# Gated linear attention in batches and a merge by branches, in a hybrid mixer block

## The chip, the cores and the metric

One core of a Trainium2 chip runs the whole block. The metric is the device time of one execution in microseconds (us), the median over several runs. Below, PE is TensorE (matmuls), ACT is ScalarE, DVE is VectorE, POOL is GpSimd, SP is SyncE, which here only issues loads.

## The reference, cut to what matters

512 tokens of width 1024 go through one layer. The input norm gives `h`; four branches are computed from `h @ w_in`, merged, and followed by an MLP.

```
merged = 0
for i in range(4):
    gate = sigmoid(h @ w_gate[i] + b_gate[i])               # 1024 x 1024 each
    merged = merged + gate * (branches[i] @ w_branch_up[i]) # 256 x 1024 each
x = x + rms_norm(merged @ w_out, norm_mix_post)
# branch 2, gated linear attention: 4 heads, 8 chunks of 64 tokens, 32 key channels, 64 value channels
attn = where(lower, q_in @ k_in.T, 0)          # within a chunk
o_c = attn @ v_c + q_in @ state                # per chunk
state = state * decay[:, None] + k_tail.T @ v_c
```

Branch 0 is a gated delta rule, branch 1 latent attention, branch 2 gated linear attention, branch 3 attention with forget gates ("forgetting attention"). Branches 0 and 2 end in a norm per head times an output gate. Everything is float32.

## The kernel before, in words

Activations are kept transposed, [128 channels, 512 tokens]. To keep float32 accuracy with faster matmuls, both sides of a projection are split into a high and a low part (`split`, L149 on ACT and L150 on DVE), and `mm3` (L246) makes three matmuls: hi*hi, hi*lo, lo*hi. A projection of 1024 channels onto 128 (`proj`) so has 24 matmuls of 128x512 columns, into one of two PSUM banks `acc`. Weights come through SP's queue into `raw` (four buffers of [128, 1024]) and are split into `whi`, `wlo` (three buffers each). Other PSUM work takes turns in six banks, b0 to b5; `banks["ring"]` says which of them a stage may use, and `ps_sm` takes the next one.

The order on each engine is not the order of the code. A scheduler at build time takes, for each engine, the earliest line of the program that its own model of the time finds ready, with a free buffer. So work that stands late in the code, as the gates' projections, fills TensorE while an earlier stage waits.

The stages, in the order of the code: input norm; projections for branch 0; its recurrence; other projections; two of the merge's gates (`gates(G0)`); inverses of 32x32 blocks; output gates; forgetting attention (`attention`, L757 logits, L770 transposes, L777 times v, L779 copy out); gated linear attention (L790 to L843); latent attention; merge (L933 to L962); output projection, second norm, MLP.

In gated linear attention, L801 makes `k_in q_in` for each head (32 rows of the array; one head after the other, each masked by L803 into a tile `gat`). Then a loop over the eight chunks follows: for an even chunk L820 multiplies `gat` with v (64 columns a head), L824 spreads the state of the four heads to a block matrix on DVE, L827 multiplies it with `q_in`, L832 makes `k v` of the chunk (64 rows, 32 columns a head), L838 updates the state on DVE, and after an odd chunk L842 copies the outputs. A float32 matmul is issued as two TensorE instructions, so counts in the trace are twice those of the code.

The merge first splits all eight outputs `brT` into hi and lo (`brh`, `brl`). Then it goes over the eight blocks m of 128 output channels. For each it has four gates (`gates`, at most 11 ahead, five places in `keep`, six in `gp2`), loads the block's columns of all four `w_branch_up` (512 KB), and for each branch makes six matmuls into a bank, multiplies by the gate (L957, DVE), and adds on POOL (L959, L961). The sum is split into `mh`, `ml`. `rowproj` then loads `w_out` in eight blocks of 128 rows; its blocks 3 to 6 are split into buffers that lie where the merge's memory was, so they wait for `ph1.close()`.

Of the kernel before, what the change touches and what calls it, by code (L numbers as in the profile page):

```python
# [25 lines left out]
NGATE = (5, 6)  # L26
# [9 lines left out]
# columns of w_in  # L36
# [5 lines left out]
# columns of the constants  # L42
# [10 lines left out]
# columns of the per-channel vectors  # L53
# [4 lines left out]
def constants():  # L58
# [19 lines left out]
    # rows of the row tile: 0-3 q norm, 4-7 k norm, 36-39 chunk tail, 96-99 fox, 100-103 gate, 104-107 beta  # L78
# [27 lines left out]
    # rows of the stacked row tile: 0-31 norms hi, 32-63 norms lo, 64-95 gates lo, 96-127 gates hi  # L106
# [14 lines left out]
def hybrid_mixer_kernel(ctx, tc, I, out):  # L121
# [8 lines left out]

    def ps_acc():
        return psp.tile([P, 512], F32, name="acc", tag="acc", bufs=2)
# [19 lines left out]
    # the tensor engine's clock rises with use  # L152
# [46 lines left out]
    def sumsq(ps, lhsT, src, t, first, last):  # L199
        """ps += lhsT.T @ src**2, the square in two parts"""  # L200
        sq, hi, lo = t("sq"), t("sqh", F32R), t("sql", F32R)
        act.activation(out=sq, in_=src, func=AF.Square)
        split(hi, lo, sq)
        pe.matmul(out=ps, lhsT=lhsT, rhs=hi, start=first, stop=False)
        pe.matmul(out=ps, lhsT=lhsT, rhs=lo, start=False, stop=last)
# [88 lines left out]
    def rows_4k(c0, a):  # L294
        """[128, 4, 256] of w_in"""
# [25 lines left out]
    def fslot(i, name, dt=F32):  # L321
        """the places of the keys and queries of FOX, then of GLA's tiles, then of the branches' high parts"""
# [8 lines left out]
    def bslot(name, dt=F32):  # L331
        return keep.tile([P, S], dt, name=name, tag="brT", bufs=8)

    brT = {i: [bslot("brT") for p in range(2)] for i in (0, 2)}
# [7 lines left out]
    def selector(kind, i):  # L342
        """one-hot rows against all 128 outputs (kind 0, 1: head i) or each half's head (2, 3: pair i)"""
# [9 lines left out]
    # token layout: gla_v | fox_v  # L353
# [11 lines left out]
    def silu(dst, src):  # L365
        """dst = src * sigmoid(src)"""
# [6 lines left out]
    def softplus(dst, z, rows):  # L373
        """dst = max(z, 0) + log1p(exp(-|z|)) on the given partitions"""
# [4 lines left out]
        # series for small arguments  # L379
# [26 lines left out]
    # rows: 0-31 kpe, 32-63 kpe with its halves swapped, 64-79 gla_lr, 96-99 fox_f, 100-103 dn_a, 104-107 dn_b  # L406
# [48 lines left out]
    # A^T and (q k)^T per head, [key, (tile, query)]  # L455
# [35 lines left out]
    # decayed q, transposed, in the place of q  # L491
# [8 lines left out]
    # token layout: k times beta and decay, v times beta (in the places of k and v), k times tail decay  # L500
# [14 lines left out]
    def gate_proj(bi, zc0):  # L515
        """silu of the projected output gate"""
        for p, wt in enumerate(stat_tiles(w_in, zc0, 256)):
            psz = proj(wt, hh, hl)
            z = brT[bi][p]
# [29 lines left out]
    gts = []  # L549

    def gslot(n):
        """the place of the n-th gate"""
        early = n % sum(NGATE) < NGATE[0]
        return (keep if early else gp2).tile([P, S], F32, name="gate", tag="gate0" if early else "gate1",
                                             bufs=NGATE[not early])

    def gates(upto):
        for n in range(len(gts), min(upto, 4 * KD)):
            m, i = n // 4, n % 4
            ps = proj(w_split(raw_cols(I["w_gate"][0, i], P * m)), hh, hl)  # L560
            g = gslot(n)
            with tc.high_priority():
                act.activation(out=g, in_=ps, func=AF.Exp, scale=-1.0, bias=vecn(8 * i + m))
            act.activation(out=g, in_=g, func=AF.Ln, bias=1.0)
            act.activation(out=g, in_=g, func=AF.Exp, scale=-1.0)
            gts.append(g)

    gates(G0)
    # inverses of the diagonal 32x32 blocks of I + A^T, half of a block's columns to a partition
    half = [slice(C * e, C * e + C) for e in range(2)]  # L570
    za = [bslot("za")[:, 0:256 * (e + 1)].rearrange("p (s c) -> p s c", c=16) for e in range(2)]
# [25 lines left out]
    XC = [bslot("XC").rearrange("p (g c) -> p g c", c=32) for z in range(2)]  # L597
# [7 lines left out]
    brT.update({i: [bslot("brT") for p in range(2)] for i in (3, 1)})  # L605
    # (I + A)^-1 transposed, from the inverses of its 32-blocks
# [4 lines left out]
    def times_at(h, src):  # L611
        """the chunks' products, one above the other"""
# [37 lines left out]
    # recurrence over chunks; the state is kept block diagonal for each pair of heads  # L650
# [43 lines left out]
    def head_norm(bi, gain_row, oT):  # L694
        """rms norm over each head's channels, times the gate"""
        for p in range(2):
# [6 lines left out]
            dve.tensor_tensor(out=brT[bi][p], in0=brT[bi][p], in1=sq, op=ALU.mult)  # L703

    # gated linear attention: gates, decayed queries and keys
# [45 lines left out]
    def attention(ap, p, qT, kT, rows, scale, mask, vt, bi, sb, tb):  # L751
        for j in range(NT):
# [26 lines left out]
            act.copy(out=brT[bi][p][:, j * P:n], in_=psb[:, 0:P])  # L779

    # forgetting attention: 64 channels, then the rows (f_q, 1) against (1, -f_k)
# [5 lines left out]
    gp = fp  # L787
    GT = ("oG0", "gat0", "gat1", "gat2", "gat3", "oG1")

    def gt_(name):  # L790
        return fslot(GT.index(name), name)

    at = []
    for h in range(H):
        hs = slice(32 * h, 32 * h + 32)
        a_ = gt_(f"gat{h}")
        pool.memset(a_, 0.0)
        ps = ps_sm()
        for j in range(NT):
            js = slice(j * P, (j + 1) * P)  # L800
            pe.matmul(out=ps[:, js], lhsT=k_in[hs, js], rhs=q_in[hs, js], start=j == 0, stop=j == NT - 1,  # L801
                      skip_group_check=True, tile_position=(32 * h, 0))
        dve.copy_predicated(out=a_.rearrange("p (j c) -> p j c", c=P),  # L803
                            mask=cv("inc").bitcast(I32).unsqueeze(1).broadcast_to([P, NT, P]),
                            data=ps.rearrange("p (j c) -> p j c", c=P))
        at.append(a_)

    oG = [gt_("oG0"), gt_("oG1")]
# [3 lines left out]
    for n in range(NCH):  # L812
        j, o = n // 2, n % 2
        rs = slice(C * o, C * o + C)
        cur, nxt = Sg[n % 2], Sg[(n + 1) % 2]
        if o == 0:
            pso = ps_sm()
            for h in range(H):
                p, e = h // 2, h % 2
                pe.matmul(out=pso[C * e:C * e + C, p * P:(p + 1) * P], lhsT=vtok[0][:, j, C * h:C * h + C],  # L820
                          rhs=at[h][:, j * P:(j + 1) * P], start=h < 2, stop=False, skip_group_check=True)
        if n > 0:
            sm_ = gp.tile([P, 256], F32, name="Smask", tag="Smask", bufs=2)
            dve.tensor_tensor(out=sm_.rearrange("p (h c) -> p h c", c=C), in0=cur.unsqueeze(1).broadcast_to([P, H, C]),  # L824
                              in1=cv("bd32").rearrange("p (h c) -> p h c", c=C), op=ALU.mult)
            for p in range(2):
                pe.matmul(out=pso[:, p * P + C * o:p * P + C * o + C], lhsT=sm_[:, p * P:(p + 1) * P],  # L827
                          rhs=q_in[:, C * n:C * n + C], start=False, stop=o == 1 and p == 1, skip_group_check=True)
        if n < NCH - 1:
            psk = ps_sm()  # L830
            for h in range(H):
                pe.matmul(out=psk[32 * h:32 * h + 32, 0:C], lhsT=ktg[rs, j * P + 32 * h:j * P + 32 * h + 32],  # L832
                          rhs=vtok[0][rs, j, C * h:C * h + C], start=True, stop=True, skip_group_check=True,
                          tile_position=(C * o, 32 * h))
            if n == 0:
                dve.tensor_copy(out=nxt, in_=psk[:, 0:C])
            else:
# [291 lines left out]
```

## Time and profile before

| | |
|---|---|
| three runs, us | 912.97, 908.45, 916.18 |
| median, us | 912.97 |
| profiled execution: its span, us | 906.0 |
| TensorE busy | 891.2 us, 98% |
| VectorE, ScalarE, GpSimd busy | 49%, 43%, 13% |
| chain that ended last | 94% TensorE |
| moved by DMA | 83.30 MB |

The profile gives the profiled execution's time as its span, from its first to its last instruction; the median of the runs is 7.0 us above it. In the chain, 57% of the span are the matmuls of L246 into `acc` and 24% those into the other banks.

### The profile page before, as it was taken

The page shows a single profiled execution, that of the slowest core. Times are in us where ns is not written, and L with a number is a line of the kernel's source. Part 1 is how long each engine was busy: PE and PEld are TensorE (multiplying, and loading weights), DVE is VectorE, ACT ScalarE, POOL GpSimd, SP SyncE. Part 2 cuts the span into 40 slices and gives each one's busy share as a digit, 9 for nine tenths or more (in the row PEclk, how much of TensorE's full clock was granted, in tenths as well). Part 3 has the DMA queues.
Part 4 walks back from the last instruction along what each step waited for, and adds up shares of the span by engine and source line. Part 5 has one row for each costly group of instructions (what it writes and reads, how often), then busy time and mean ns, then how long its engine had stood idle before and what let it go on. Part 6 is the DMA issues. An engine that isn't in the chain of part 4 may idle for free.

```text
span 906.0 us, 11146 instructions
## 1 busy us (share of the span) xinstructions
PE 891.2 (98%) x4407; PEld 724.1 (80%) x4407; DVE 443.2 (49%) x717; ACT 393.4 (43%) x685; POOL 113.5 (13%) x96
## 2 busy tenths in 40 slices
PE   7999999999999999999999999999999999999997
PEld 6987788877667777888888789888888888888885
DVE  6378797436866775443336467322222233333324
ACT  6346453423886764445543355333222333222222
POOL 3100020100000002221124200422332200000000
PEclk9999999999999999999999999999999999999999
DMA  7333244501121012333333732333333333323202
GB/s 261 105 94 93 58 93 110 118 24 39 55 60 47 26 53 67 112 93 94 93 95 92 237 87 70 115 96 94 93 95 102 130 116 94 93 93 94 93 1 93
DMA packets 123699, 83.30 MB, mean 92 GB/s; under 512 B 19488, under 2 KB 115760, under 8 KB 123648
## 3 DMA queue, kind: packets, MB, share of 16 engines
q1 hardware_dynamic: 117696, 77.03, 29.5%
q10 hardware_dynamic: 5696, 4.73, 1.7%
q0 software_dynamic: 256, 0.85, 0.3%
q8 instruction: 34, 0.56, 0.2%
q14 instruction: 17, 0.14, 0.1%
HBM read 79.69 MB, written 2.88 MB: 91 GB/s over the span
## 4 chain that ended last, share of the span: by engine, by line
PE 94%; DVE 2%; ACT 1%; DMA 1%; POOL 1%; issue 0%; ACTq 0%; DVEq 0%; POOLq 0%
PE acc L246 57%; PE b L246 24%; PE b L757 2%; PE b L777 2%; PE b L278 1%; PE b L469 1%; PE b L770 1%; DMA raw<-in_w_out_dram 1%; PE b L616 1%; PE b L673 1%; PE b L801 1%; PE b L678 1%; POOL gate L959 1%; PE b L665 1%; PE b L646 0%
## 5 line engine op out<-in xcount | busy, mean ns | idle before, releaser
L150 DVE TENSOR_TENSOR wlo<-raw,whi 128x1024 fp32r<-128x1024 f32 x134 | 172.8, 1293 | 264.2 <-ACT whi L149 263.9
L149 ACT CAST whi<-raw 128x1024 fp32r<-128x1024 f32 x136 | 142.4, 1050 | 272.4 <-PE acc L246 238.7
L246 PE MATMUL acc<-hl,whi 128*128 128x512 f32 x416 | 165.4, 398 | 0.0
L246 PE MATMUL acc<-hh,whi 128*128 128x512 f32 x416 | 165.2, 397 | 0.0
L246 PE MATMUL acc<-hh,wlo 128*128 128x512 f32 x416 | 164.1, 394 | 0.0
L246 PE MATMUL acc<-h2l,whi 128*128 128x512 f32 (+1 forms) x240 | 91.8, 383 | 0.0
L246 PE MATMUL acc<-h2h,whi 128*128 128x512 f32 (+1 forms) x240 | 91.8, 382 | 0.0
L246 PE MATMUL acc<-h2h,wlo 128*128 128x512 f32 (+1 forms) x240 | 91.7, 382 | 0.0
L246 PEld LDWEIGHTS acc<-hl,whi 128*128 128x128 f32 x416 | 78.4, 188 | 16.6 <-issue 1.2
L246 PEld LDWEIGHTS acc<-hh,whi 128*128 128x128 f32 x416 | 78.2, 188 | 16.2 <-issue 1.1
L246 PEld LDWEIGHTS acc<-hh,wlo 128*128 128x128 f32 x416 | 78.2, 188 | 15.6 <-issue 0.4
L246 PE MATMUL b<-wlo,whi 128*128 128x512 f32 x192 | 74.8, 389 | 0.0
L246 PE MATMUL b<-whi 128*128 128x512 f32 x192 | 74.8, 389 | 0.0
L246 PE MATMUL b<-whi,wlo 128*128 128x512 f32 x192 | 74.7, 390 | 0.0
L246 PEld LDWEIGHTS acc<-h2h,whi 128*128 128x128 f32 x240 | 45.1, 188 | 8.8
L246 PEld LDWEIGHTS acc<-h2h,wlo 128*128 128x128 f32 x240 | 45.1, 188 | 8.7
L246 PEld LDWEIGHTS acc<-h2l,whi 128*128 128x128 f32 x240 | 45.1, 188 | 8.6
L959 POOL TENSOR_TENSOR gate<-gate 128x512 f32<-128x512 f32 x16 | 22.6, 1416 | 189.2 <-DVE gate L957 189.2
L246 PEld LDWEIGHTS b<-whi,wlo 128*128 128x128 f32 x192 | 36.1, 188 | 7.8 <-DVE wlo L150 0.4
L246 PEld LDWEIGHTS b<-wlo,whi 128*128 128x128 f32 x192 | 36.1, 188 | 7.5
L246 PEld LDWEIGHTS b<-whi 128*128 128x128 f32 x192 | 36.1, 188 | 7.4
L1035 POOL TENSOR_TENSOR u<-u 128x512 f32<-128x512 f32 x16 | 25.7, 1604 | 110.3 <-ACT u L1034 110.1
(312 smaller groups left out, 1413.8 us busy)
## 6 DMA issues: line engine op xcount, KB each, us to landing
raw<-in_w_gate_dram SPq DMA_DIRECT2D x32, 512.0 KB, 3.8
raw<-in_w_mlp_in_dram SPq DMA_DIRECT2D x32, 512.0 KB, 4.2
raw<-in_w_mlp_out_dram SPq DMA_DIRECT2D x32, 512.0 KB, 3.5
raw<-in_w_in_dram SPq DMA_DIRECT2D x23, 512.0 KB, 3.9
raw<-in_w_branch_up_dram SPq DMA_DIRECT2D x8, 512.0 KB, 3.9
raw<-in_w_out_dram SPq DMA_DIRECT2D x8, 512.0 KB, 3.5
x_t<-in_x_dram SPq DMA_DIRECT2D x4, 512.0 KB, 7.5
x<-in_x_dram ACTq DMA_DIRECT2D x1, 2048.0 KB, 12.3
```

The costliest lines, as they stand in the source:

```text
L149: act.copy(out=hi, in_=src)
L150: eng.tensor_tensor(out=lo, in0=src, in1=hi.bitcast(F32), op=ALU.subtract)
L246: pe.matmul(out=ps, lhsT=a, rhs=b, start=first and i == 0, stop=last and i == 2, skip_group_check=True)
L278: pe.transpose(out=ps[:, k * P:(k + 1) * P], in_=(src if late else sq)[:, ks], identity=ident)
L469: pe.matmul(out=ps2[:, js], lhsT=qkvT[2 + p][r, js], rhs=qkvT[rhs_i + p][r, js], start=j == 0, stop=j == NT - 1, skip_group_check=True)
L616: pe.matmul(out=pv[:, j], lhsT=av[h][:, j], rhs=src[:, j], start=j == 0, stop=j == NT - 1, skip_group_check=True)
L665: pe.matmul(out=psv[rs, p * P:(p + 1) * P], lhsT=wT[p][:, C * n:C * n + C], rhs=cur[:, p], start=p == 0, stop=p == 1, skip_group_check=True)
L673: pe.matmul(out=pso[:, p * P + C * o:p * P + C * o + C], lhsT=cur[:, p], rhs=qd[p][:, C * n:C * n + C], start=o == 0 and p == 0, stop=Fals ...
L757: pe.matmul(out=ps[:, 0:n], lhsT=qT[e][0:rows, j * P:n], rhs=kT[e][0:rows, 0:n], start=True, stop=True)
L777: pe.matmul(out=psb[C * e:C * e + C, 0:P], lhsT=vt(k, 2 * p + e), rhs=pts[e][:, k * P:(k + 1) * P], start=k == 0, stop=k == j)
L959: pool.tensor_tensor(out=g, in0=g, in1=gts[4 * m + i - 1], op=ALU.add)
L1035: pool.tensor_tensor(out=dst, in0=dst, in1=dst, op=ALU.mult)
```

## The change

Gated linear attention: L801's matmuls are made for two heads at a time, the heads taking turns, into two banks; then all products `k v` of chunks 0 to 6 into two banks (even chunks in one, odd ones in the other); then all sixteen products with `gat` into b0 and b1; then the chunks' states follow each other on DVE, which reads the products where they are, and only L827's counterpart is left on TensorE in the loop. `in_order` ties the matmuls of a batch to this order among themselves (it adds no wait on the chip). Outputs are copied for four chunks at once.

Outputs of branches are written as hi and lo where they arise (`br_parts`), into places fixed by `HOME`; `brT` and the later split are gone. The merge goes branch by branch, in the order 0, 3, 2, 1, over eight accumulators `acc[m]`: the first branch's gates are the accumulators; gates of the other branches have three buffers. `w_branch_up` is loaded per branch and pair of blocks (256 KB). Up-projections of branch 0 use bank b5 alone, those of 3 and 2 four banks, those of 1 six. For the last branch the addition is on DVE. Comments and docstrings are dropped.

```diff
+    def in_order(made):
+        for a, b in zip(made, made[1:]):
+            tc.add_manual_dep(b.ins, a.ins.name, mybir.DependencyInfo(mybir.DependencyClass.NoSync,
+                                                                      mybir.DependencyReason.DATA), reason="in_order")
...
+    HOME = {(0, 0): (bslot, 4), (0, 1): (bslot, 6), (3, 0): (bslot, 0), (3, 1): (fslot, 0),
+            (2, 0): (fslot, 4), (2, 1): (fslot, 2), (1, 0): (bslot, 2), (1, 1): (fslot, 6)}
+    def br_parts(i, p):
+        f, n = HOME[i, p]
+        br_hl[i, p] = f(n, "brh", F32R), f(n + 1, "brl", F32R)
+        return br_hl[i, p]
...
+    def gate(i, m):
+        if i == ORDER[0]:
+            g = acc[m] = (keep if m < NACC else gp2).tile([P, S], F32, name="acc", tag=f"acc{m}")
+        else:
+            g = gp2.tile([P, S], F32, name="gate", tag="gate", bufs=3)
+        ps = proj(w_split(raw_cols(I["w_gate"][0, i], P * m)), hh, hl)
...
+    for m in range(G0):
+        gate(ORDER[0], m)
...
     def head_norm(bi, gain_row, oT):
-            dve.tensor_tensor(out=brT[bi][p], in0=brT[bi][p], in1=sq, op=ALU.mult)
+            pr = tmp("pr")
+            dve.tensor_tensor(out=pr, in0=zg[bi][p], in1=sq, op=ALU.mult)
+            split(*br_parts(bi, p), pr)
...
     def attention(ap, p, qT, kT, rows, scale, mask, vt, bi, sb, tb):
+        bh, bl = br_parts(bi, p)
...
-            act.copy(out=brT[bi][p][:, j * P:n], in_=psb[:, 0:P])
+            act.copy(out=bh[:, j * P:n], in_=psb[:, 0:P])
+            dve.tensor_tensor(out=bl[:, j * P:n], in0=psb[:, 0:P], in1=bh[:, j * P:n].bitcast(F32), op=ALU.subtract)
...
+    for p in range(2):
+        pss, made = [ps_sm(), ps_sm()], []
+        for e in range(2):
+            a_ = fslot((4, 5, 2, 3)[2 * p + e], "gat")
+            pool.memset(a_, 0.0)
+            at.append(a_)
         for j in range(NT):
             js = slice(j * P, (j + 1) * P)
+            for e in (1, 0):
+                h = 2 * p + e
+                hs = slice(32 * h, 32 * h + 32)
+                made.append(pe.matmul(out=pss[e][:, js], lhsT=k_in[hs, js], rhs=q_in[hs, js], start=j == 0,
+                                      stop=j == NT - 1, skip_group_check=True, tile_position=(32 * h, 0)))
+        in_order(made)
...
+    psk, made = [ps_sm(), ps_sm()], []
+    for n in range(NCH - 1):
+        j, o = n // 2, n % 2
+        rs = half[o]
+        for h in range(H):
+            hs = slice(32 * h, 32 * h + 32)
+            made.append(pe.matmul(out=psk[o][hs, C * j:C * j + C], lhsT=ktg[rs, j * P + 32 * h:j * P + 32 * h + 32],
+                                  rhs=vtok[0][rs, j, C * h:C * h + C], start=j == 0, stop=n >= NCH - 3,
+                                  skip_group_check=True, tile_position=(C * o, 32 * h)))
+    in_order(made)
+
+    psO, made = [ps_sm("b0"), ps_sm("b1")], []
+    for j in range(NT):
+        for h in range(H):
+            p, e = h // 2, h % 2
+            q0 = 256 * (j % 2) + p * P
+            made.append(pe.matmul(out=psO[j // 2][C * e:C * e + C, q0:q0 + P], lhsT=vtok[0][:, j, C * h:C * h + C],
+                                  rhs=at[h][:, j * P:(j + 1) * P], start=j % 2 == 0 and h < 2, stop=False,
+                                  skip_group_check=True))
+    in_order(made)
...
+    for n in range(1, NCH):
+        j, o = n // 2, n % 2
+        cur, prev = Sg[n % 2], Sg[(n - 1) % 2]
+        add = psk[(n - 1) % 2][:, C * ((n - 1) // 2):C * ((n - 1) // 2) + C]
+        if n == 1:
+            dve.tensor_copy(out=cur, in_=add)
+        else:
+            dve.scalar_tensor_tensor(out=cur, in0=prev, scalar=cdg[:, n - 1:n], in1=add, op0=ALU.mult, op1=ALU.add)
...
+        for p in range(2):
+            q0 = 256 * (j % 2) + p * P + C * o
+            pe.matmul(out=psO[j // 2][:, q0:q0 + C], lhsT=sm_[:, p * P:(p + 1) * P],
+                      rhs=q_in[:, C * n:C * n + C], start=False, stop=n % 4 == 3 and p == 1, skip_group_check=True)
...
+    for n, i in enumerate(ORDER):
+        banks["ring"] = (("b5",), ("b0", "b1", "b4", "b5"), ("b0", "b1", "b4", "b5"), ("b0", "b1", "b2", "b3", "b4", "b5"))[n]
+        for c in range(KD // 2):
+            g = {m: acc[m] if n == 0 and m < G0 else gate(i, m) for m in (2 * c, 2 * c + 1)}
+            rv = raw_tile()[:, 0:512].rearrange("p (k c) -> p k c", k=2)
+            sp.dma_start(out=rv, in_=I["w_branch_up"][0][i].rearrange("(k p) c -> p k c", p=P)[:, :, 256 * c:256 * c + 256])
+            hi, lo = w_split(rv)
+            for m in (2 * c, 2 * c + 1):
+                ps = ps_sm()
+                ms = slice(P * (m % 2), P * (m % 2) + P)
+                for k in range(2):
+                    mm3(ps, hi[:, k, ms], lo[:, k, ms], *br_hl[i, k], k == 0, k == 1)
+                dve.tensor_tensor(out=g[m], in0=ps, in1=g[m], op=ALU.mult)
+                if n in (1, 2):
+                    pool.tensor_tensor(out=acc[m], in0=acc[m], in1=g[m], op=ALU.add)
+                elif n == 3:
+                    dve.tensor_tensor(out=g[m], in0=acc[m], in1=g[m], op=ALU.add)
+                    split(mh[:, m], ml[:, m], g[m])
```

## Rows read from the trace of the kernel before

**Rows 1.** The page: engines' busy us, share of the span, instructions.

```profile
PE 891.2 (98%) x4407; PEld 724.1 (80%) x4407; DVE 443.2 (49%) x717; ACT 393.4 (43%) x685; POOL 113.5 (13%) x96
```

**Rows 2.** The chain that ended last, dense stretch: start us, us, what.

```profile
374.16 21.76 PE acc L246 x96
```

**Rows 3.** Windows: stretch, its length, busy us and instructions of each engine, clock, DMA.

```profile
280.00:300.00 20.00, 20.00 (x175) 15.20 (x176) 10.42 (x29) 12.29 (x31) 0.00 (x0) 1.00 0.10 28
...
350.00:494.00 144.00, 144.00 (x637) 119.31 (x636) 60.96 (x59) 71.07 (x97) 30.63 (x19) 1.00 0.33 99
```

**Rows 4.** TensorE's timeline, 288 to 291 us: start, us, group of instructions.

```profile
288.13 0.65 PE L820 MATMUL b<-gat,gv 128*64 128x128 f32 x6
288.71 0.66 PE L827 MATMUL b<-gqk,Smask 128*128 128x64 f32 x4
289.30 0.43 PE L820 MATMUL b<-gat,gv 128*64 128x128 f32 x2
289.66 0.50 PE L246 MATMUL b<-lhi,llo 128*128 128x512 f32 x1
290.00 0.28 PE L246 MATMUL b<-lhi 128*128 128x256 f32 x1
...
290.24 0.28 PE L246 MATMUL b<-lhi,llo 128*128 128x256 f32 x1
290.44 0.32 PE L832 MATMUL b<-gv,gB 64*32 64x64 f32 x8
290.69 0.50 PE L246 MATMUL acc<-hl,whi 128*128 128x512 f32 x1
```

**Rows 5.** TensorE's timeline: first, one whole and last run of this part.

```profile
227.89 0.48 PE L801 MATMUL b<-gqk 32*128 32x128 f32 x2
...
272.56 1.15 PE L801 MATMUL b<-gqk 32*128 32x128 f32 x8
...
296.16 0.32 PE L832 MATMUL b<-gv,gB 64*32 64x64 f32 x8
```

**Rows 6.** Groups by line: busy us, mean ns of one, idle before.

```profile
L957 DVE TENSOR_TENSOR gate<-b,gate 128x512 f32<-128x512 f32 x32 | 21.8, 688 | 11.0 <-PE b L246 10.8
L758 DVE TENSOR_TENSOR b<-b,cst 128x128 f32<-128x128 f32 x32 | 9.5, 296 | 9.4 <-PE b L757 8.8
L824 DVE TENSOR_TENSOR Smask<-Sg,cst 128x256 f32<-128x256 f32 x7 | 3.0, 423 | 0.2
L838 DVE SCALAR_TENSOR_TENSOR Sg<-Sg,cdg,b 128x64 f32<-128x64 f32 x6 | 1.7, 280 | 7.5 <-PE b L832 7.5
```

**Rows 7.** Gates taken out of PSUM from 217 to 340 us; issues of SP's queue.

```profile
L563 ACT ACTIVATE gate<-acc,vneg x9: 677/682/689, 222.7 to 336.5; 128x512 f32<-128x512 f32 x9
263.07 0.37 SPq L949 DMA_DIRECT2D raw<-in_w_branch_up_dram  x1
273.35 42.74 SPq L220 DMA_DIRECT2D raw<-in_w_gate_dram  x4
```

**Rows 8.** Timelines of all engines at the end of the merge, 498 to 522 us.

```profile
498.89 0.40 PE L246 MATMUL b<-brh,wlo 128*128 128x512 f32 x1
503.84 1.29 POOL L961 TENSOR_TENSOR gate<-gate 128x512 f32<-128x512 f32 x1
502.64 7.49 SPq L992 DMA_DIRECT2D raw<-in_w_out_dram  x2
507.46 3.91 ACT L149 CAST whi<-raw 128x1024 fp32r<-128x1024 f32 x4 [1.68 <-DVE ml L150]
518.38 1.05 ACT L149 CAST whi<-raw 128x1024 fp32r<-128x1024 f32 x1 [7.01 <-DMA raw<-in_w_out_dram]
518.50 0.39 PE L246 MATMUL b<-whi,ml 128*128 128x512 f32 x1
519.48 0.50 PE L246 MATMUL b<-whi,mh 128*128 128x512 f32 x1 [0.59 <-ACT whi L149]
520.74 0.50 PE L246 MATMUL b<-wlo,mh 128*128 128x512 f32 x1 [0.76 <-DVE wlo L150]
```

More of the change, by code (lines that the diff above doesn't have):

```diff
@@ L25 @@
 DFF = 4 * D
-NGATE = (5, 6)
+NACC = 5
+ORDER = (0, 3, 2, 1)
 NHALF = 4
@@ L329, in kslot, with bslot @@
         return prp.tile([P, S], dt, name=name, tag=tag or name, bufs=bufs)
-    def bslot(name, dt=F32):
-        return keep.tile([P, S], dt, name=name, tag="brT", bufs=8)
-    brT = {i: [bslot("brT") for p in range(2)] for i in (0, 2)}
+    def bslot(i, name, dt=F32):
+        return keep.tile([P, S], dt, name=name, tag=f"br{i}")
+    zg = {i: [bslot(i + p, "zg") for p in range(2)] for i in (0, 2)}
+    HOME = {(0, 0): (bslot, 4), (0, 1): (bslot, 6), (3, 0): (bslot, 0), (3, 1): (fslot, 0),
+            (2, 0): (fslot, 4), (2, 1): (fslot, 2), (1, 0): (bslot, 2), (1, 1): (fslot, 6)}
+    br_hl = {}
+    def br_parts(i, p):
+        f, n = HOME[i, p]
+        br_hl[i, p] = f(n, "brh", F32R), f(n + 1, "brl", F32R)
+        return br_hl[i, p]
     pelr = kslot("pelr")
@@ L518, in gate_proj @@
             psz = proj(wt, hh, hl)
-            z = brT[bi][p]
+            z = zg[bi][p]
             act.copy(out=z, in_=psz)
@@ L548, in hybrid_mixer_kernel @@
         act.copy(out=lat[-1], in_=ps)
[L549 to L568, printed above, removed]
+    acc = {}
+    def gate(i, m):
[4 more added lines that the diff above has]
+        ps = proj(w_split(raw_cols(I["w_gate"][0, i], P * m)), hh, hl)
+        with tc.high_priority():
+            act.activation(out=g, in_=ps, func=AF.Exp, scale=-1.0, bias=vecn(8 * i + m))
+        act.activation(out=g, in_=g, func=AF.Ln, bias=1.0)
+        act.activation(out=g, in_=g, func=AF.Exp, scale=-1.0)
+        return g
+    for m in range(G0):
+        gate(ORDER[0], m)
     half = [slice(C * e, C * e + C) for e in range(2)]
-    za = [bslot("za")[:, 0:256 * (e + 1)].rearrange("p (s c) -> p s c", c=16) for e in range(2)]
+    za = [bslot(4 + e, "za")[:, 0:256 * (e + 1)].rearrange("p (s c) -> p s c", c=16) for e in range(2)]
     z0 = slot("z0", "wT", 2).rearrange("p (s c) -> p s c", s=32)
@@ L596, in hybrid_mixer_kernel @@
         pool.tensor_tensor(out=a_, in0=a_, in1=cv("off32").unsqueeze(1).broadcast_to([P, NT, P]), op=ALU.mult)
-    XC = [bslot("XC").rearrange("p (g c) -> p g c", c=32) for z in range(2)]
+    XC = [bslot(6 + z, "XC").rearrange("p (g c) -> p g c", c=32) for z in range(2)]
     for z in (1, 0):
@@ L603, in hybrid_mixer_kernel @@
                            in1=cv("blk2").unsqueeze(1).unsqueeze(3).broadcast_to([P, H * NT, 2, 32]), op=ALU.mult)
-    brT.update({i: [bslot("brT") for p in range(2)] for i in (3, 1)})
     wT = []
@@ L787, in hybrid_mixer_kernel @@
     gp = fp
-    GT = ("oG0", "gat0", "gat1", "gat2", "gat3", "oG1")
-    def gt_(name):
-        return fslot(GT.index(name), name)
     at = []
[L794 to L798, printed above, removed]
+    for p in range(2):
[4 more added lines that the diff above has]
+            at.append(a_)
@@ L799, in hybrid_mixer_kernel @@
         for j in range(NT):
             js = slice(j * P, (j + 1) * P)
[L801 to L806, printed above, removed]
@@ L808, in hybrid_mixer_kernel @@
-    oG = [gt_("oG0"), gt_("oG1")]
+            for e in (1, 0):
[4 more added lines that the diff above has]
+        in_order(made)
+        for e in range(2):
+            dve.copy_predicated(out=at[2 * p + e].rearrange("p (j c) -> p j c", c=P),
+                                mask=cv("inc").bitcast(I32).unsqueeze(1).broadcast_to([P, NT, P]),
+                                data=pss[e].rearrange("p (j c) -> p j c", c=P))
@@ new lines, in hybrid_mixer_kernel @@
+    in_order(made)
[8 more added lines that the diff above has]
+    in_order(made)
+    oG = [fslot(6 + p, "oG") for p in range(2)]
@@ L811, in hybrid_mixer_kernel @@
         Sg.append(gp.tile([P, C], F32, name=f"Sg{i}"))
-    for n in range(NCH):
+    for n in range(1, NCH):
         j, o = n // 2, n % 2
[L814 to L825, printed above, removed]
-            for p in range(2):
[L827 to L837, printed above, removed]
-                dve.scalar_tensor_tensor(out=nxt, in0=cur, scalar=cdg[:, n:n + 1], in1=psk[:, 0:C],
-                                         op0=ALU.mult, op1=ALU.add)
-        if o == 1:
-            for p in range(2):
-                act.copy(out=oG[p][:, j * P:(j + 1) * P], in_=pso[:, p * P:(p + 1) * P])
@@ new lines, in hybrid_mixer_kernel @@
+        cur, prev = Sg[n % 2], Sg[(n - 1) % 2]
[4 more added lines that the diff above has]
+            dve.scalar_tensor_tensor(out=cur, in0=prev, scalar=cdg[:, n - 1:n], in1=add, op0=ALU.mult, op1=ALU.add)
+        sm_ = gp.tile([P, 256], F32, name="Smask", tag="Smask", bufs=2)
+        dve.tensor_tensor(out=sm_.rearrange("p (h c) -> p h c", c=C), in0=cur.unsqueeze(1).broadcast_to([P, H, C]),
+                          in1=cv("bd32").rearrange("p (h c) -> p h c", c=C), op=ALU.mult)
@@ new lines, in hybrid_mixer_kernel @@
+        for p in range(2):
+            q0 = 256 * (j % 2) + p * P + C * o
+            pe.matmul(out=psO[j // 2][:, q0:q0 + C], lhsT=sm_[:, p * P:(p + 1) * P],
+                      rhs=q_in[:, C * n:C * n + C], start=False, stop=n % 4 == 3 and p == 1, skip_group_check=True)
+        if n % 4 == 3:
+            i = j // 2
+            pv = psO[i].rearrange("q (j p c) -> q j p c", j=2, p=2)
+            for p in range(2):
+                act.copy(out=oG[p][:, 256 * i:256 * i + 256].rearrange("q (j c) -> q j c", j=2), in_=pv[:, :, p])
@@ L936, in hybrid_mixer_kernel @@
     ml = m_tile("ml", F32R)
-    br_hl = {}
-    for n, (i, p) in enumerate((i, p) for i in (0, 3, 2, 1) for p in range(2)):
-        hi = fslot(n, "brh", F32R)
-        lo = bslot("brl", F32R) if n else tmp("brl", F32R)
-        split(hi, lo, brT[i][p])
-        br_hl[i, p] = hi, lo
-    banks["ring"] = ("b0", "b1", "b2", "b3", "b4", "b5")
-    for m in range(KD):
-        gates(4 * m + sum(NGATE))
-        rv = raw_tile().rearrange("p (k c) -> p k c", k=KD)
-        sp.dma_start(out=rv, in_=I["w_branch_up"][0].rearrange("i (k p) c -> p (i k) c", p=P)[:, :, P * m:P * m + P])
-        hi, lo = w_split(rv)
-        for i in range(4):
-            ps = ps_sm()
-            for k in range(2):
-                bh, bl = br_hl[i, k]
-                mm3(ps, hi[:, 2 * i + k], lo[:, 2 * i + k], bh, bl, k == 0, k == 1)
-            g = gts[4 * m + i]
-            dve.tensor_tensor(out=g, in0=ps, in1=g, op=ALU.mult)
-            if i % 2:
-                pool.tensor_tensor(out=g, in0=g, in1=gts[4 * m + i - 1], op=ALU.add)
-        g = gts[4 * m + 3]
-        pool.tensor_tensor(out=g, in0=g, in1=gts[4 * m + 1], op=ALU.add)
-        split(mh[:, m], ml[:, m], g)
+    for n, i in enumerate(ORDER):
[16 more added lines that the diff above has]
+                    split(mh[:, m], ml[:, m], g[m])
     ph1.close()
```

## The prediction

> **What bounds the kernel now.** I read the page's busy shares first, then the cost of one dense matmul in the chain of waits, then the windows by stage, then TensorE's timeline around the work that is changed, and last the end of the merge. TensorE is busy 98% of the span [rows 1]. The next engine, VectorE, has 49%. "Busy" is modelled, so I need a price of one matmul: 96 of the 128x512 kind take 21.76 us in the dense stretch [rows 2], 0.227 us each. Between 350 and 494 us TensorE issues 637 of them, 0.226 us each, at a granted clock of 1.00 (the upper level, 2.4 GHz), and nothing is lost there [rows 3]. In the stretch from 280 to 300 us, where gated linear attention runs, 175 instructions fill a "busy" 20 us [rows 3]; the loss has to be inside that stretch.
>
> The timeline shows where [rows 4]. I compare the end of a group (start plus duration) with the end of the group before it. The lone 128x512 matmul at 289.66 ends at 290.16, the group before it at 289.73: 0.43 us for a matmul worth 0.227, so 0.20 is lost. The one at 290.69 ends at 291.19 after 290.76: again 0.43. The group of 4 at 288.71 (128x64, 0.11 each) loses 0.14, and the eight of L832 at 290.44 end 0.24 after the group before them although their own spacing comes to about 0.08: 0.16. Each time the active rows x columns change (128*64 to 128*128, 128*128 to 64*32 and back). Where the form stays, as from 290.00 to 290.24, nothing is lost. A change of form so costs about 0.18 us (mean of 0.20, 0.20, 0.14, 0.16). Gated linear attention is cut into short runs between other work: eight runs of L801 from 227.89 to 278.01, seven of L820 and seven of L832, the last at 296.16 [rows 5]. That is 22 runs, two ends each, one end shared: 43 changes, 43 x 0.18 = 7.7 us.
>
> **The change part by part.**
>
> *Batches.* The number of TensorE instructions in this part stays: L801 32, L820 32, L832 56, L827 28. The states no longer need TensorE between chunks: all products k v come first, VectorE carries the state. So there are two batches of L801, one of L832 and one of L820; L827 has the full 128*128 form. At least 4 runs (8 changes) are left; attention on the forget gates has priority and cut the eight runs of L801 out of four heads, so I take 6 runs, 12 changes: 31 x 0.18 = **-5.7 us**. Bounds: 8 changes left give -6.3; if the runs are cut as often as now and only the waits for the state go (13 changes fewer), -2.3.
>
> *Alternating row tiles.* Within a batch of L801 the two heads, on different rows, take turns and write different banks. Now eight of one head take 1.15 us [rows 5], 0.11 apart, 32 x 0.11 = 3.5 us. The trace has no turns between rows. Its nearest row is L820, whose heads take turns between column halves: six in 0.65 us although the first of them alone lasts 0.32 [rows 4], so two go side by side. By that row half of 3.5 us goes, **-1.8 us**, and I take it. Bounds: 0 if rows do not overlap, and +2.5 us if each of 14 turns cost 0.18 like a change of form. The Trainium skill ("TensorE: Matmul & The Clock Gate", Part 3) has K=32 matmuls in distinct row groups run side by side, 3.07 times as fast with four; two groups at most halve the 3.5 us, so the sum by it would be no larger.
>
> *State.* Seven steps of 0.28 and 0.42 us on VectorE (L838, L824 [rows 6]), 4.9 us; now they are spread at least from 288.1 to 296.2 [rows 4, 5]. What hides them is projections on TensorE; nothing on the path.
>
> *Where outputs are split.* Four ScalarE copies and four subtractions of 128x512 move behind the head norms; the eight outputs of the attentions get 16 subtractions of 128x128 out of PSUM (about 0.30 each by L758 [rows 6]) in place of 4 whole splits. The added wait: the next step's transposes need the same bank, so every step waits some 0.45 us longer with its hand-off, 16 x 0.45 = 7.2 us on the chain of attentions. The cover is gate projections, 24 x 0.227 = 5.44 us each. Now nine of them fill 217 to 340 us [rows 7]. Afterwards, until the first attention ends, six gates and eight up-projections of branch 0 (1.36 us each) and three more gates can run, 6 x 5.44 + 8 x 1.36 + 3 x 5.44 = 60 us, and those of branches 3 and 2 follow. I take 0; +7.2 if the cover is gone.
>
> *Up-projections of branch 0* all use one bank. Between two of them lie the product (0.69 us, L957 [rows 6]) and a hand-off, some 1.0 us, 8 x 1.0 = 8 us if nothing else is ready. Gates are; 0, with +8 as bound. TensorE's 192 up-projection matmuls and 256 x 3 gate matmuls stay as they are. The weights come as 16 pieces of 256 KB instead of 8 of 512 KB, SP's queue has eight more issues, and with 33% DMA share in the dense stretch [rows 3] that is 0. With only three gate buffers the fourth gate is written 10.9 us of TensorE after the first was used; the product and GpSimd's addition (0.69 [rows 6], 1.29 [rows 8]) are done by then. 0.
>
> *End of the merge.* Now the last up-projection's matmul is over at 499.29; then come the products and three additions on GpSimd, the last of them until 505.13, and the split [rows 8]. The split of w_out's blocks 3 to 6 needs the memory that this frees, and starts at 507.46, 2.33 behind. The raw buffer for the last block comes free with the first of these splits; SP's last issue is over at 510.13, ScalarE waits 7.01 us for that load until 518.38, and TensorE waits with it: matmuls that end at 518.89, 519.98 and 521.24 with 0.23 due between them lose 0.86 + 1.03 = 1.9 us. After the change a product and VectorE's addition, 0.69 each by L957, follow the matmul, behind the neighbour's about 0.7 later: 499.29 + 0.2 + 1.4 + 0.7 = 501.6, and the splits start 2.33 behind that, at 503.9, 3.5 us earlier than now. The last block is then ready before TensorE gets to it: **-1.9 us** (bound 0, if that load is late for another reason). Next in line is nothing: matmuls of other blocks are ready.
>
> Sum: -5.7 - 1.8 - 1.9 = -9.4 us on this profile's span of 906.0, so 896.6. The median run, 912.97, lies 7.0 above that span; I carry this over: **903.6 us**, 1.03% less. About 1% is what a measurement here can tell from no change, so the forecast lies on that border.
>
> **The rivals.**
> 1. *The batches are cut up as before.* The scheduler mixes by readiness, and the priority of the forget attention cut single heads into two and three runs [rows 5]; against it, a batch needs two banks, of which that attention uses one, so it starts when most of that work is over. Only -2.3 and the end's -1.9 are left, and turns between rows give nothing: 908.8 us. Chance 0.22.
> 2. *Missing filler, slower.* Place: 217 to 300 us. Branch 0's up-projections need bank b5, and so do both batches of L801 and the products k v. Their weights sit in raw and hi/lo buffers until then: now the first w_branch_up block is loaded at 263.07 [rows 7], long before the last branch is there, and holds one buffer; afterwards there are four such blocks early. If they hold the buffers, gates cannot be prepared and TensorE stands still: five of nine gates not run in time, 27 us, 903.6 + 27 = 931 us. It decides once three blocks are split before the first up-projection has run. Against it: behind the block of 263.07, four gate loads still went out from 273.35 on [rows 7], so a block that waits does not stop the gates, and the nine gates ran. Chance 0.09.
> 3. *The turns between rows cost instead of overlapping* and the attention chain loses half its cover: 903.6 + 4.3 + 3.6 = 911.5 us. Chance 0.10.
> 4. *More than I count.* The longer supply of filler also removes cuts between the attentions' own short runs; 20 changes fewer, 900 us. Chance 0.14.
>
> **How the numbers follow.** Forecast 0.45 (900 to 907), rivals 0.22, 0.09, 0.10, 0.14. Runs scatter from 908.45 to 916.18, so a median may be off by 3. Faster by over 1% means below 903.8: half of the forecast (0.23), rival 4 (0.14) and some scatter of the others (0.06), together 0.43. Slower by over 1%, above 922.1: rival 2, 0.09. Within: 0.48. The range reaches from rival 4 less 3 (897) to rival 3 plus 2.5 (914); what is left out is rival 2 and little of the others.
>
> **What would show it.** TensorE's timeline: L801, L832 and L820 in 4 to 8 runs; eight of L801 in about 0.6 us instead of 1.15; no wait for the last w_out block; gate projections between the attentions until they end, and no idle time before up-projections. It is wrong if these runs stay short and many, if TensorE waits for a bank or for weights between 217 and 300 us, or if the dense stretch from the end of the attentions to w_out has losses that it has not now.

## The result, and the profile after

The changed kernel takes 922.79 us (median of 4 runs, 922.60 to 927.33) where the kernel before took 913.40 on the same chip (908.45 to 916.18). By the ratio on record it is 1.27% more (1.0127, interval 1.0084 to 1.0169). Ratios are taken over all fast runs; they need not equal the quotient of two medians (here 1.0103), since the runs of one kernel fall in groups some 5 us apart. The forecast was 903.6 us with a range to 914. It went as rival 2 said, missing filler, which had a chance of 0.09. The profiled execution spans 920.8 us, 14.8 more than before.

The busy line of the changed kernel's page comes first (as rows 1):

```profile
PE 896.4 (97%) x4407; PEld 725.6 (79%) x4407; DVE 443.6 (48%) x745; ACT 393.0 (43%) x685; POOL 98.0 (11%) x88
```

TensorE has the same 4407 matmuls; its share only falls from 98% to 97% [rows 1], which tells next to nothing. The windows by stage do tell. Their columns: stretch, length, busy us and instructions of TensorE, of its weight loads, VectorE, ScalarE, GpSimd, then the granted clock, DMA share, GB/s. The kernel before, four stretches that were not shown yet (280 to 300 is in rows 3):

```profile
220.00:240.00 20.00, 20.00 (x91) 15.51 (x90) 16.15 (x34) 16.55 (x34) 0.00 (x0) 1.00 0.27 80
240.00:260.00 20.00, 19.72 (x104) 13.20 (x103) 15.82 (x41) 17.83 (x44) 1.06 (x2) 1.00 0.09 26
260.00:280.00 20.00, 19.87 (x117) 13.09 (x115) 14.54 (x34) 14.21 (x36) 1.05 (x2) 1.00 0.27 80
...
300.00:320.00 20.00, 20.00 (x100) 14.02 (x100) 14.96 (x38) 16.01 (x38) 0.00 (x0) 1.00 0.18 52
```

The changed kernel, the same stretches and the dense one:

```profile
220.00:240.00 20.00, 18.00 (x73) 13.17 (x71) 13.72 (x29) 14.37 (x28) 0.00 (x0) 0.91 0.22 66
240.00:260.00 20.00, 15.88 (x53) 8.32 (x51) 15.06 (x38) 15.59 (x38) 1.06 (x2) 0.63 0.13 40
260.00:280.00 20.00, 19.62 (x102) 12.72 (x102) 12.53 (x38) 13.02 (x36) 0.52 (x1) 0.94 0.10 27
280.00:300.00 20.00, 19.58 (x207) 15.55 (x207) 14.16 (x32) 9.27 (x20) 0.52 (x1) 1.00 0.05 14
300.00:320.00 20.00, 16.52 (x74) 11.46 (x74) 15.71 (x38) 13.87 (x33) 0.00 (x0) 1.00 0.22 62
...
363.00:507.00 144.00, 144.00 (x637) 119.29 (x636) 57.77 (x66) 70.27 (x101) 23.94 (x16) 1.00 0.32 97
```

The dense stretch has its 637 matmuls in 144 us as before, only 13 us later. The time is lost between 220 and 320 us. There TensorE issues 73 + 53 + 102 + 207 + 74 = 509 instructions; before they were 91 + 104 + 117 + 175 + 100 = 587 (one that lies across an edge is counted on both sides). The 78 that are missing must run later; at 0.226 us each [rows 3] that is an estimate of 17.6 us. ScalarE and VectorE are not busier there: added up, ScalarE works 66.1 us against 76.9 before, VectorE 71.2 against 71.9. The clock fell with the work: 0.63 in the mean from 240 to 260 us, between the levels of 1.2 and 2.4 GHz, after the pauses that TensorE's timeline shows (start, us, group; in brackets the idle time before it and what ended it):

```profile
231.49 0.71 PE L253 MATMUL acc<-hh,whi 128*128 128x512 f32 x1 [1.81 <-ACT whi L156]
...
239.81 0.48 PE L253 MATMUL acc<-hh,wlo 128*128 128x512 f32 x1
243.17 0.91 PE L774 MATMUL b<-fk,fq 66*128 66x384 f32 x2 [2.88 <-ACT prob L782]
...
261.05 0.63 PE L253 MATMUL acc<-hh,whi 128*128 128x512 f32 x1
261.47 0.63 PE L253 MATMUL acc<-hl,whi 128*128 128x512 f32 x1
...
280.98 0.71 PE L818 MATMUL b<-gqk 32*128 32x128 f32 x8
...
288.65 0.79 PE L833 MATMUL b<-gv,gB 64*32 64x64 f32 x56
289.37 1.75 PE L843 MATMUL b<-gat,gv 128*64 128x128 f32 x28
291.41 0.66 PE L864 MATMUL b<-gqk,Smask 128*128 128x64 f32 x4 [0.29 <-DVE Smask L860]
...
304.19 0.50 PE L253 MATMUL b<-brh,whi 128*128 128x512 f32 x1 [0.16 <-ACT rs L714]
```

Between 239.81 and 261.05 no gate projection's matmul ran: apart from six sums for norms (L211, L212) only the attention on the forget gates was on TensorE, and TensorE waited for it, 2.88 us of it in one piece for exponentials. The first matmul of branch 0's up-projections came at 304.19. ScalarE's timeline shows when weights were split (128x1024 is a gate's, 128x512 one of w_branch_up's):

```profile
170.50 0.62 ACT L156 CAST whi<-raw 128x512 fp32r<-128x512 f32 x1 [2.47 <-PE acc L253]
...
222.43 0.62 ACT L156 CAST whi<-raw 128x512 fp32r<-128x512 f32 x1 [4.61 <-PE acc L253]
230.41 1.03 ACT L156 CAST whi<-raw 128x1024 fp32r<-128x1024 f32 x1
257.80 1.03 ACT L156 CAST whi<-raw 128x1024 fp32r<-128x1024 f32 x1
305.42 0.61 ACT L156 CAST whi<-raw 128x512 fp32r<-128x512 f32 x1
```

Two blocks of w_branch_up were split at 170.50 and 222.43 and held two of the three hi/lo pairs until 304.19. One pair was left for all gates: a split of gate weights at 230.41, the next at 257.80, and none more until after 305. The groups of the gates' first exponential between 217 and 300 us (us of one, first and last start), changed kernel:

```profile
L577 ACT ACTIVATE acc<-acc,vneg x3: 670/672/683, 223.0 to 240.4; 128x512 f32<-128x512 f32 x3
```

and the kernel before:

```profile
L563 ACT ACTIVATE gate<-acc,vneg x5: 677/682/689, 222.7 to 282.4; 128x512 f32<-128x512 f32 x5
```

The end of the merge answers to rows 8; timelines of all engines of the changed kernel:

```profile
515.50 0.40 PE L253 MATMUL b<-brh,wlo 128*128 128x512 f32 x1
...
516.59 1.28 DVE L982 TENSOR_TENSOR gate<-acc,gate 128x512 f32<-128x512 f32 x2
...
521.17 3.89 ACT L156 CAST whi<-raw 128x1024 fp32r<-128x1024 f32 x4 [2.63 <-DVE ml L157]
...
532.19 1.05 ACT L156 CAST whi<-raw 128x1024 fp32r<-128x1024 f32 x1 [7.13 <-DMA raw<-in_w_out_dram]
...
532.53 0.39 PE L253 MATMUL b<-whi,mh 128*128 128x512 f32 x1
532.76 0.40 PE L253 MATMUL b<-wlo,mh 128*128 128x512 f32 x1
```

ScalarE still waits 7.13 us for the last w_out block, but TensorE has matmuls of other blocks all the while, and its two waits of 0.59 and 0.76 us [rows 8] are gone. The splits of w_out start 521.17 - 515.90 = 5.3 us behind the last up-projection's matmul; before it was 8.2 [rows 8].

### The profile page after: what moved, and what is told of

It reads as the page before. It is cut to its first block, busy times and chain, and to the rows that moved or that the text cites. A ratio compares the mean times of both kernels' runs of the same rounds, so it can differ in the third digit from the quotient of the medians.

```text
span 920.8 us, 11219 instructions
## 1 busy us (share of the span) xinstructions
PE 896.4 (97%) x4407; PEld 725.6 (79%) x4407; DVE 443.6 (48%) x745; ACT 393.0 (43%) x685; POOL 98.0 (11%) x88
## 3 DMA queue, kind: packets, MB, share of 16 engines
HBM read 79.69 MB, written 2.88 MB: 90 GB/s over the span
## 4 chain that ended last, share of the span: by engine, by line
PE 94%; ACT 3%; DVE 2%; DMA 1%; issue 1%; DVEq 0%; ACTq 0%; POOL 0%; POOLq 0%
PE acc L253 56%; PE b L253 25%; PE b L774 2%; PE b L794 2%; PE b L787 1%; PE b L285 1%; PE b L487 1%; PE b L630 1%; PE b L687 1%; DMA cst<-in_cst_dram 1%; PE b L692 1%; PE b L679 1%; PE b L660 0%; PE b L652 0%; PE b L211 0%
## 5 line engine op out<-in xcount | busy, mean ns | idle before, releaser
L157 DVE TENSOR_TENSOR wlo<-raw,whi 128x1024 fp32r<-128x1024 f32 (+1 forms) x142 | 169.7, 1198 | 294.5 <-ACT whi L156 294.3
L980 POOL TENSOR_TENSOR acc<-acc,gate 128x512 f32<-128x512 f32 x16 | 23.9, 1515 | 160.1 <-ACT gate L579 85.9
```

The lines of the kernel that those rows point to most:

```text
L157: eng.tensor_tensor(out=lo, in0=src, in1=hi.bitcast(F32), op=ALU.subtract)
L980: pool.tensor_tensor(out=acc[m], in0=acc[m], in1=g[m], op=ALU.add)
```

## The experiments

Theory 1: branch 0's up-projections, emitted between the gates but unable to run, hold what the gates need. Theory 2: the attention has more work on ScalarE and VectorE (16 subtractions, later splits). Theory 3: the batches of gated linear attention themselves cost. Ratios are against the kernel before on the same chip, with 95% intervals; "instructions" are TensorE's from 220 to 320 us, added up from windows as above.

| run | ratio | interval | instructions |
|---|---|---|---|
| before | 1 | | 587 |
| changed | 1.0127 | 1.0084 to 1.0169 | 509 |
| e1 up-projections on other banks | 1.0109 | 1.0082 to 1.0136 | 541 |
| e2 gates first | 0.9959 | 0.9939 to 0.9979 | 591 |
| e3 gated linear attention alone | 0.9938 | 0.9911 to 0.9964 | 622 |
| e4 merge alone | 1.0264 | 1.0222 to 1.0306 | 476 |
| e5 before, two pairs held | 1.0255 | 1.0213 to 1.0296 | 486 |
| e6 gates first, other banks | 0.9936 | 0.9910 to 0.9962 | 602 |
| e7 changed, whole splits | 1.0125 | 1.0068 to 1.0182 | 535 |
| e8 as e6, whole splits | 0.9931 | 0.9902 to 0.9960 | 601 |
| e9 as e6, one block at the eighth gate | 0.9919 | 0.9890 to 0.9948 | 603 |
| e10 as e6, one block at the seventh gate | 0.9912 | 0.9878 to 0.9947 | 609 |

**e1.** Another place for eight up-projections, nothing else:

```
-                ps = ps_sm()
+                ps = ps_acc() if n == 0 else ps_sm()
```

> Only branch 0's eight up-projections are changed: they use the two accumulator banks of the projections instead of b5. Theory 1 (they wait for b5, which gated linear attention holds, and their weights hold two of the three hi/lo buffers, so that gates cannot be prepared): the products of branch 0 start at about 240 us instead of 307, the loss between 230 and 310 us falls from about 28 to about 15 us, and the run takes 905 to 912 us. Theory 2 (the weights' splits come late because ScalarE and VectorE are full with the attention's work, of which there is more): the products start early, but the gates between 240 and 300 us are as few as now, and the time stays within 918 to 925.

The products did start early, at 241.8 us, and the time did not come back. TensorE's timeline shows why:

```profile
219.97 0.49 PE L774 MATMUL b<-fk,fq 66*128 66x128 f32 x2
228.70 1.12 PE L753 MATMUL b<-cst,gz 128*128 128x128 f32 x4 [8.24 <-DVE gz L746]
...
234.42 0.79 PE L253 MATMUL acc<-brh,whi 128*128 128x512 f32 x1 [0.20 <-ACT brh L156]
```

No gate ran between 220 and 242 us, though the weights of two were split, at 202.82 and 219.25: these gates come behind two up-projections that want the same two banks, and the up-projections could not start before branch 0's output was there, at 234.42. From 220 to 240 us TensorE issued 23 instructions at a clock of 0.56. The hold-up has moved, from the hi/lo pairs to the accumulator banks and 20 us forward. Neither theory had this form in its numbers: 919.56 us lies in the range of theory 2, with two gates from 240 to 300 us for one in the changed kernel, so this run by itself does not decide between the two.

**e2.** The order of emission alone:

```
     for n, i in enumerate(ORDER):
...
+        for m in range(G0, KD if n == 0 else G0):
+            gate(i, m)
         for c in range(KD // 2):
-            g = {m: acc[m] if n == 0 and m < G0 else gate(i, m) for m in (2 * c, 2 * c + 1)}
+            g = {m: acc[m] if n == 0 else gate(i, m) for m in (2 * c, 2 * c + 1)}
```

> Program order alone: branch 0's six remaining gates are emitted ahead of its up-projections, b5 stays. Theory 1 in its form with the buffers (weights of blocked up-projections hold them): all six gates are over before 300 us (now four of them), and the run takes 905 to 912 us. If the bank itself is the whole trouble (what is missing is the up-projections as filler): the gates only come earlier and the stretch behind them is empty, 915 to 923. Theory 2 (ScalarE and VectorE full): 918 to 925.

905.63 us against 908.75, 1.7% less than the changed kernel's ratio, with the same instructions, banks and splits. Between 217 and 300 us all six gates are done:

```profile
L577 ACT ACTIVATE acc<-acc,vneg x6: 682/688/707, 224.1 to 295.7; 128x512 f32<-128x512 f32 x6
```

**e3 and e4** take the change apart. e3 is the kernel before with the new lines of gated linear attention (from `at = []` to `head_norm(2, ...)`), e4 the changed kernel with the old ones (its tiles in the slots that the new merge leaves free). e3:

```
-    for h in range(H):
...
-        ps = ps_sm()
+    for p in range(2):
+        pss, made = [ps_sm(), ps_sm()], []
...
+    psk, made = [ps_sm(), ps_sm()], []
+    for n in range(NCH - 1):
...
```

and e4 the same lines the other way round.

> The kernel before with the batched gated linear attention alone; the merge, its splits and the gates are those of before. By the prediction's terms -5.7 for changes of form and -1.8 for the alternating rows: 905 to 908 us where the kernel before has 913. If the batches themselves cost the time (two banks held for longer, VectorE's state chain at the end), 915 to 923.

> The changed kernel with the gated linear attention of before (same order, one bank at a time, states through TensorE). If the loss is the merge's (theory 1 or 2): 925 to 932 us, the changed kernel plus the 5 to 8 us that the batches save. If the loss is the batches': 910 to 914.

e3: 904.45 us against 908.75; by the ratio 0.62%, 5.6 us (3.3 to 8.1), come from the batches alone. e4: the merge alone costs 2.64%, 24 us. Theory 3 falls. The two don't add up: e4 and the changed kernel differ by 1.37%, 12.5 us, where 5 to 8 were expected, so the batches saved more in the kernel that lacks work than in the one that has it, by little more than the intervals allow for chance. Which part of it does that was not tried. In e3's timeline the alternating rows stand beside the 1.15 us for eight in rows 5:

```profile
277.31 1.16 PE L806 MATMUL b<-gqk 32*128 32x128 f32 x16
```

**e5.** The suspected cause by itself, in the kernel before: two blocks of w_branch_up loaded and split ahead of the nine gates. Bank b5, the attention's splits and the merge are those of before.

```
+    held = [up_block(m) for m in range(2)]
     for m in range(KD):
         gates(4 * m + sum(NGATE))
...
+        hi, lo = held[m] if m < len(held) else up_block(m)
```

> The kernel before, with one thing of the change: two w_branch_up blocks are loaded and split ahead of the nine gates, and so hold two of the three hi/lo pairs until the last branch is there. Bank b5, the gated linear attention, the merge and all splits of the branches are those of before. Theory 1 (held hi/lo pairs keep the gates from being prepared): 1.5 to 3% slower than before, TensorE with pauses between 220 and 300 us and a granted clock under 0.8 in one stretch there. Theory 2 (more work on ScalarE and VectorE in the attention) and theory 3 (bank b5): no change, within 0.5%.

2.55% slower, about as much as the whole new merge costs in e4. The two loads (timeline of SP's queue), the windows, and the first matmul with those weights:

```profile
162.38 5.11 SPq L948 DMA_DIRECT2D raw<-in_w_branch_up_dram  x2
```

```profile
220.00:240.00 20.00, 15.86 (x58) 11.56 (x56) 13.26 (x26) 13.06 (x25) 0.00 (x0) 0.83 0.16 46
240.00:260.00 20.00, 15.86 (x44) 8.68 (x44) 13.12 (x35) 13.35 (x35) 0.53 (x1) 0.53 0.15 40
```

```profile
336.26 0.48 PE L246 MATMUL b<-brh,whi 128*128 128x512 f32 x1
```

It has the same picture as the changed kernel, pauses, a clock of 0.53 and ScalarE less busy than before, without one line of the change. The Trainium skill ("Perfetto Trace Analysis", Optimization Strategy) says that a gap which repeats on the engine that should be saturated can mean too little memory for the next tile, by buffer count or size. This case agrees: one pair instead of three, 2.55%. The dose is not that of the changed kernel, where the pairs were held until 304.19 and not until 336.26.

**e6 and e8.** Gates first as in e2 with the banks of e1 (e6); and with the attentions' outputs split whole (e8, by e7's edit below):

```
+        for m in range(G0, KD if n == 0 else G0):
+            gate(i, m)
...
-                ps = ps_sm()
+                ps = ps_acc() if n == 0 else ps_sm()
```

> Gates first, and the up-projections of branch 0 on the projections' two banks. In e2 the stretch from 280 to 320 us still lost 4.3 us of idle time at TensorE, with the up-projections waiting for b5 until 301 us. Theory 1: with both the order and the bank mended the products start at 285 to 295 us and 3 to 5 us more come back: 0.5 to 1.0% faster than before (e2: 0.4%). If the bank matters nowhere: as e2, 0.2 to 0.6% faster.

> e6 with the attentions' outputs split whole as in e7. With gates and up-projections as cover the 16 subtractions cost nothing (the prediction's term): the same as e6 within 0.3%. If they are on the path even so: 0.3 to 0.8% less time than e6.

With the gates ahead the bank of e1 does no harm. The products start at 298.3 us, later than expected, and 0.64% instead of 0.41% is gained; the intervals overlap, so what b5 costs is not shown. Of the stretches where e2 stood idle, e6 has 0.63 and 1.77 us left:

```profile
280.00:300.00 20.00, 19.37 (x202) 16.23 (x203) 13.18 (x33) 11.78 (x28) 0.00 (x0) 1.00 0.01 2
300.00:320.00 20.00, 18.23 (x86) 12.30 (x85) 18.10 (x46) 10.57 (x26) 0.00 (x0) 1.00 0.36 104
```

**e7** does to the changed kernel what e8 does to e6:

```
-            act.copy(out=bh[:, j * P:n], in_=psb[:, 0:P])
-            dve.tensor_tensor(out=bl[:, j * P:n], in0=psb[:, 0:P], in1=bh[:, j * P:n].bitcast(F32), op=ALU.subtract)
+            act.copy(out=raw_o[:, j * P:n], in_=psb[:, 0:P])
+        split(bh, bl, raw_o)
```

> The changed kernel, but the attentions' outputs are copied out whole and split once at the end of a pair (4 splits of 128x512) instead of 16 subtractions of 128x128 out of PSUM. Theory 2 (the longer attention chain is the loss): 0.5 to 0.8% less time than the changed kernel, which is 0.5 to 0.8% slower than before. Theory 1: the loss stays, 1.0 to 1.5% slower than before.

e7 has the changed kernel's ratio and e8 that of e6: theory 2 has no part that can be measured. e7's one profiled execution was 4.2 us shorter (916.6 against 920.8) and issued 26 instructions more from 220 to 320 us, and the two intervals leave room for a part of some 0.7% in the kernel without cover. The 0.5 to 0.8% that theory 2 expected is so not excluded there by e7 alone; against theory 2 as the cause of the loss stands e2, which has all 16 subtractions and is faster than before.

**e9 and e10** put one block back between the gates:

```
+            if n == 0:
+                for m in range(len(acc), (7, 8, 8, 8)[c]):
+                    gate(i, m)
```

(e10: 6 in place of 7.)

> e6 with the first w_branch_up block moved ahead of the eighth gate: one hi/lo pair at most is held, and two up-projections can run between the attentions on the forget gates, from 240 us on (in e6 none ran before the gated linear attention was over, and 300 to 320 us had 1.8 us of idle time). Theory 1 (one held pair does no harm, early filler helps): as e6 or up to 2 us less, 0.6 to 0.9% faster than before. If a single held pair already costs: slower than e6 by 2 us or more.

> As e9, with the first block ahead of the seventh gate and the others behind the eighth: the pair is held from earlier on. Theory 1: as e6 within 2 us, 0.5 to 0.9% faster than before. If a single held pair already costs, more so here than in e9: 0.4% faster at most.

903.40 and 902.75 us against 911.81. One pair held for a short time does no harm: the first block was split at 235.46 in e9 and 230.50 in e10, its matmuls began at 253.03 and 241.23, with one gate of branch 0 (e9) or two (e10) still to be split. A single pair held from 170 us on, ahead of all gates, was not tried, so it is not shown that the damage begins with the second. Nor does a second pair harm at any time: in e2 two blocks were split while b5 was not yet free, and held their pairs to about 300 us, but all six gates of branch 0 were split by then:

```profile
236.47 1.04 ACT L156 CAST whi<-raw 128x1024 fp32r<-128x1024 f32 x1
...
262.85 0.64 ACT L156 CAST whi<-raw 128x512 fp32r<-128x512 f32 x1
264.56 0.62 ACT L156 CAST whi<-raw 128x512 fp32r<-128x512 f32 x1
```

What costs is pairs held while gates still need them. These are the fastest versions that ran, 0.8 and 0.9% faster than before; between e6, e9, e10 and e3 the intervals do not decide.

## Why the prediction was wrong

- **The failed step** is the cover: "Between two of them lie the product and a hand-off ... Gates are [ready]; 0", and the 60 us of filler counted under the splits. I counted how much filler there is, not whether it can be made ready. Each block of `w_branch_up` whose two up-projections wait keeps a hi/lo pair; with two such blocks, one pair is left for all gates. In the kernel before, two pairs held until 336 us cost 2.55%, 23 us (e5); in the changed kernel the order that causes it is worth 1.68%, 15 us (e2), about twice the bound of +8 that I gave.
- **Rival 2 had the mechanism and the place.** Its price, 27 us, is near the 24 of e4; the changed kernel as a whole came out 19 us above the forecast. Two details were off. Two split blocks were enough, not three. And b5 is not what decides: the same loss is there in e5 without it, and it goes in e2 with it.
- **The reason that kept its chance at 0.09 was misread.** That four gate loads went out behind the block of 263.07 [rows 7] says nothing of a held pair, because by the order of the splits that block held a raw buffer and no pair. The kernel before loads nine gates and then the block; in the changed kernel, where the forms tell them apart, weights are split in the order of their loads. By that order the nine gates' splits run from 169.47 to 309.77, and the block's is the next, at 313.11, when the stretch is over (ScalarE's timeline of the kernel before):

```profile
231.38 1.03 ACT L149 CAST whi<-raw 128x1024 fp32r<-128x1024 f32 x1
257.18 1.04 ACT L149 CAST whi<-raw 128x1024 fp32r<-128x1024 f32 x1
...
309.77 1.03 ACT L149 CAST whi<-raw 128x1024 fp32r<-128x1024 f32 x1
...
313.11 1.05 ACT L149 CAST whi<-raw 128x1024 fp32r<-128x1024 f32 x1
```

So the kernel before had the gates first and all three pairs for them; the change gave that up, and the row could not show what it costs.

- **Batches and alternating rows:** predicted -5.7 and -1.8, together -7.5; e3 measures -5.6 (3.3 to 8.1) for both, so sign and sum hold; what each brought by itself was not measured. (31 x 0.18 is 5.6, not 5.7.) Sixteen turns take 1.16 us, (1.16 - 0.27) / 15 = 0.06 each with 0.27 for one instruction, in place of 0.11 [rows 5]; for 32 that is -1.6. The Trainium skill ("TensorE: Matmul & The Clock Gate", Part 3) has matmuls of small K in distinct row groups run side by side; the trace agrees, by nearly the half that two groups allow. L818 came in six runs, L833 in one, L843 in two: nine, where the sum had six runs and the signs to look for had 4 to 8. Eight of L818 now last 0.71 us (at 280.98).
- **State on VectorE, 0:** held. TensorE's longest wait for it was 0.29 us (L864 at 291.41).
- **Splits in attention, 0:** held where there is cover (e8 against e6); without cover e7 leaves up to some 0.7% open.
- **End of the merge, -1.9:** the waits of TensorE went as predicted (0.59 and 0.76 to none). The splits start 2.9 us earlier than before against the last matmul; 3.5 were forecast. That the last block would be split before TensorE came to it was right, though ScalarE waits for its load as long as before.
- So the terms that were to save came with some -7 us (5.6 by e3, 1.35 of waits at the end), and the one that I set at 0 cost more than they saved: 15 us by e2. With the order mended the change is 0.4 to 0.9% faster than before (e2, e6, e9, e10) where 1.03% was forecast. The prices of single experiments do not add up to the whole, as e3 and e4 show.
- What stays open: why the gate behind 240 us was split at 257.80 and not when its pair came free. ScalarE had four pauses of 0.20 to 1.38 us between 247 and 255 us; its order of work was fixed when the kernel was built. The gap is no mark of the change: the kernel before split no gate's weights between 231.38 and 257.18 either, but there the gates whose weights were split by then lasted longer: their first exponentials started at 236.88, 249.09 and 282.42, and the last of the changed kernel's at 240.38. On this reading the pairs serve as a stock for a stretch in which ScalarE splits none.

## What to carry to other kernels

Filler counts only if it can be prepared: for each stretch that relies on it, go through the buffers it passes (raw, hi/lo, accumulator bank), subtract those that waiting work already holds, and see if what is left still turns over. In a ring of buffers the order of emission decides who holds them, so work that can run goes ahead of work that waits; here moving six gates ahead of eight up-projections was worth 1.7%. When a row shows that a blocked item does no harm, ask which buffer it holds; here it was a raw buffer, and the pairs were what ran out.

## What the runs showed of the hardware

Where TensorE ran short of work its granted clock fell, and its matmuls took longer: 0.63 (240 to 260 us, after 73 instructions in the 20 us before), 0.53 in e5, 0.56 in e1; the dense matmuls of the gate at 261.05 and 261.47 are 0.42 us apart in place of 0.226. In e2, e6, e9 and e10, where TensorE's pauses add up to 0 to 0.8 us in each 20 us from 220 to 280, it was 1.00 throughout. Pauses did not always bring it down: from 300 to 320 us the changed kernel's TensorE was idle for 3.5 us at 1.00. The 56 products k v of L833 took 0.79 us in one run, where eight alone had taken 0.32 [rows 4].
